# A decoder layer on one Trainium2 core: the MLP's first product as seven half-block products, with weight sums made by adding DMAs

## The chip, the cores and the metric

The kernel runs on one core of a Trainium2 chip. The metric is device microseconds of one execution. In texts and rows PE is TensorE (PEld its weight loads), DVE is VectorE, ACT is ScalarE, POOL is GpSimd and SP is SyncE.

## What is computed

One layer of a hybrid decoder over 512 tokens of width 1024, all in float32: a norm, one wide input projection, sliding-window attention and gated linear attention side by side, their gated merge, an output projection and a residual, then a gated MLP. The change is in the MLP:

```
h = rmsnorm(x, ln_ffn_g)                      # 512 x 1024
a, u = jnp.split(h @ w_ffn_in, 2, axis=-1)    # w_ffn_in 1024 x 5632; a and u 512 x 2816
a = causal_dwconv(a, conv_w, conv_b)          # width 3, along the tokens
x = x + (jax.nn.silu(a) * u) @ w_ffn_out      # w_ffn_out 2816 x 1024
```

## The kernel before

**Products.** Each float32 product is made of float32r parts. A weight chunk is split exactly into `wh` (ACT, L257) and `wl` (DVE, L258), an activation likewise into `acth` and `actl`, and `mm3` (L261) issues three matmuls for each contraction tile of 128: high by high, high by low, low by high. All matmuls are recorded at L80.

**Weights.** A unit of 1 MB goes by SP's queue into a ring `raw` of three buffers (`load`), and is split chunk by chunk into rings `wh` and `wl` of four buffers each. The main loop calls `do_split` for chunks i to i+2 and then issues chunk i's matmuls. PE keeps the order of the text; a scheduler places the instructions of DVE, ACT and POOL by their dependences.

**The MLP's first product.** In `[columns, tokens]` form: weights stationary, 512 tokens moving. A chunk is one column tile of `a` or of `u`, 8 contraction tiles deep, so 24 matmuls; there are 44 chunks, two chunks to a unit. Before it, the last half of the output projection (`mm_o1`) goes block of tokens by block of tokens, each block's norm (L279 to L284) and its transposes (`transpose_steps`, L310 on, L324 the low part) beside the next block's matmuls. The first four chunks (`ffn_first`) take the tokens in two halves of 256, 192 matmuls in all; the other 40 chunks have 960 matmuls of 512 tokens. `evac_fa` (L589 to L599) makes the convolution and the silu of an `a` tile: a memset on POOL (L591), a copy and an activation on ACT (L592, L595), two multiply-adds on DVE (L596, L597), a table lookup on ACT (L86). `evac_fu` (L602) multiplies by the `u` tile into `gT`, eight-KiB slots of four tiles each.

**The MLP's second product.** `fo_chunk(j)` splits `gT(j)` (L640, L641) and accumulates 22 chunks into eight banks (tokens by columns). The last `TAIL` = 4 chunks go bank by bank, so that each bank's addition of the residual (L671) and its store lie beside the next bank's matmuls.

Of the kernel before, what the change touches and what calls it, by code (L numbers as in the profile page):

```python
# [27 lines left out]
STAGES = (32, 8, 2, 1)    # sub-blocks, four to a group; the last ones in pairs  # L28
NEG = -1.0e30


@with_exitstack
def hybrid_trunk(ctx: ExitStack, tc: tile.TileContext, x, ln_mix_g, w_in, q_norm_g, k_norm_g, sinks, w_gk_up,
# [9 lines left out]
    tpool = ctx.enter_context(tc.tile_pool(name="tpool", bufs=1))  # L43
    psum = ctx.enter_context(tc.tile_pool(name="psum", bufs=1, space=bass.MemoryType.PSUM))
# [9 lines left out]
    def slot(name, dt=F32):  # L54
        """An 8 KiB activation slot."""
        return apool.tile([P, 2048], dt, tag="slot", name=nm(name), bufs=10)

    def tmp(shape, name, dt=F32):
        """A short-lived tile from one of three rings, by its size."""
        n = 1  # L60
        for d in shape[1:]:
            n *= d
        tag, size, bufs = ("t0", 16, 12) if n <= 16 else ("t2", 514, 8) if n <= 514 else ("t4", 1040, 3)
# [15 lines left out]
    def matmul(ps, lhsT, rhs, start, stop):  # L79
        order(nc.tensor.matmul(ps, lhsT, rhs, start=start, stop=stop))  # L80
# [3 lines left out]
    def lookup(out, src, func, **kw):  # L84
        """An activation from a table; these keep their order, so that the tables change seldom."""
# [5 lines left out]

    def transpose(ps, src, idn):
# [54 lines left out]
    # the clock of the tensor engine comes up, and stays up, with products of the identity  # L147
# [7 lines left out]
    # the gain of the first norm goes in with the transposes, the norm itself with the products' results  # L155
# [3 lines left out]
    # per-partition parameters: rows in, one transpose  # L159
# [23 lines left out]
    def make_masks():  # L183
        low = ctile([P, P], "low")     # 1 where column <= row
# [3 lines left out]
        upp = ctile([P, P], "upp")     # 1 where column >= row  # L188
# [3 lines left out]
        slow = ctile([P, P], "slow")   # 1 where column < row  # L192
# [28 lines left out]
    def load(u):  # L221
# [4 lines left out]
        t = wpool.tile([P, 2048], F32, tag="raw", name=nm("raw"), bufs=3)[:, :n]  # L226
        t = t.rearrange("p (a b) -> p a b", a=shape[0])
        for dst, src in loads:
            nc.sync.dma_start(t[:, :, dst[0]:dst[1]], src)
        loaded[u] = t  # L230

    split, o1 = {}, []
# [5 lines left out]
    def split_steps(i):  # L238
# [4 lines left out]
        src = loaded[u][:, sl[0], sl[1]]  # L243
# [3 lines left out]
        else:  # L247
            h = wpool.tile([P, 1088], F32R, tag="wh", name=nm("wh"), bufs=4)[:, :n]
            l = wpool.tile([P, 1088], F32R, tag="wl", name=nm("wl"), bufs=4)[:, :n]
        split[i] = h, l = [t.rearrange("p (a b) -> p a b", a=shape[0]) for t in (h, l)]  # L250
        half = shape[0] // 2 if i < 2 else shape[0]
        for k in range(0, shape[0], half):
# [6 lines left out]
            yield  # L259

    def mm3(ps, lh, ll, rh, rl, first, last):  # L261
        matmul(ps, lh, rh, first, False)
        matmul(ps, lh, rl, False, False)
        matmul(ps, ll, rh, False, last)

    def rstd(ss, n, scale, name, r=None):
        """(ss * scale + eps) ** -0.5"""
# [5 lines left out]

    def act_pair(tag):
        h = apool.tile([P, KT, S], F32R, tag=tag + "h", name=nm(tag + "h"), bufs=1)
        l = apool.tile([P, KT, S], F32R, tag=tag + "l", name=nm(tag + "l"), bufs=1)
        return h, l

    def norm(src, gain, out):  # L279
        """out = rmsnorm(src) * gain"""  # L280
# [5 lines left out]
    def mix_steps(b):  # L286
        """hT[:, :, block b] = transpose(x) * gain"""
# [23 lines left out]
    def transpose_steps(h, H, L, b):  # L311
        """H + L [:, :, block b] = transpose(h)"""
        pss = [bank() for _ in range(2)]
        dst = [(slice(None), slice(4 * half, 4 * half + 4), slice(b * P, (b + 1) * P)) for half in range(2)]
# [5 lines left out]
        for d, ps in zip(dst, pss):  # L320
            nc.scalar.copy(H[d], v3(ps, 4))
            yield
        for d, ps in zip(dst, pss):
            nc.vector.tensor_sub(L[d], v3(ps, 4), H[d].bitcast(F32))  # L324
            yield
# [9 lines left out]
    def tok_major(act, key, ncols, kts, first, last, evac):  # L335
        """out[tokens, columns]: activations stationary, weights moving, one bank a block of tokens."""
# [18 lines left out]
    def col_major(act, kt, evac, ncol=1, toks=None):  # L355
        """out[columns, tokens]: weights stationary, activations moving."""
# [18 lines left out]
    act_h = lambda: hT  # noqa: E731  # L375

    # keys, values and low-rank gates of all tokens; then queries of the attention
    zk = slot("zk")[:, 0:NB * 272].rearrange("p (a b) -> p a b", a=NB)
    for u2 in range(2):
        u = unit([((0, 256), win(O_KA, O_QB, 4 * u2, 4 * u2 + 4)),  # L380
                  ((256, 272), win(O_GK, O_GA, 4 * u2, 4 * u2 + 4))], (4, 272))
# [15 lines left out]
    def tok_group(act, key, w, c0, evac):  # L397
        for u2 in range(2):
            u = unit([((0, 512), win(c0, c0 + 512, 4 * u2, 4 * u2 + 4, w))], (4, 512))
# [5 lines left out]
    def col_group(act, w, c0, ntile, evac):  # L405
        """ntile (even) column tiles from column c0; evac(j, ps)"""
        for j in range(0, ntile, 2):
            u = unit([((0, 256), win(c0 + j * P, c0 + (j + 2) * P, 0, KT, w))], (KT, 256))
# [13 lines left out]
    qk = []     # per pair of blocks: q (scaled) of the four heads, then k  # L422
# [42 lines left out]
    # a branch's projection, gated  # L465
    yaT, ybT, mT, h2T = [], [], [], []
    n_a = len(chunks)
    for j in range(0, KT, 4):
        u = unit([((0, 512), win(j * P, (j + 4) * P, 0, 4, w_a))], (4, 512))
# [22 lines left out]
    class Halves:  # L492
        """[P, KT, S] kept as two slots of four tiles each."""

        def __init__(self, pair):
            self.pair = pair

        def __getitem__(self, sl):
            p, k, t = sl
            return self.pair[k // 4][p, k % 4, t]  # L500

# [11 lines left out]
    # the first tiles take the first half of the columns while the second half of them is still on its way  # L513
    def branch_first(i):
        if i < n_rb + 3:
            return
        pss = [bank() for _ in range(4)]
# [13 lines left out]
    act_y = lambda: (Halves([ybT[0][0], ybT[1][0]]), Halves([ybT[0][1], ybT[1][1]]))  # noqa: E731  # L531
    for j in range(0, KT, 2):
        u = unit([((0, 256), win(j * P, (j + 2) * P, 0, KT, w_b))], (KT, 256))
        for c in range(2):
            chunk(u, (slice(0, KT), slice(c * P, (c + 1) * P)), (KT, P), branch_first if j < 4 else
                  col_major(act_y, KT, lambda _, ps, j=j + c: evac_b(j, ps)))

    # output projection and residual
# [572 lines left out]
```

## Time and profile before

| What | Value |
|---|---|
| median of 3 runs | 817.45 us (817.37 to 817.52) |
| span of the profiled execution | 815.8 us |
| PE, DVE, ACT, POOL busy | 99%, 55%, 40%, 13% of the span |
| DMA | 76.87 MB, mean 94 GB/s |

The page gives the span, from the first to the last instruction, and no other time for the profiled execution. The median of the runs lies 1.65 us above the span, and that is taken as what lies around it. Rows of the timeline give the start and the length of an instruction in us; a PE row's length is from issue to the modelled end, so the pace of matmuls is read from the distances of their starts.

### The profile page before, as it was taken

To read this page: it belongs to the slowest core of one execution; us is meant where nothing else is said; L and a number is where in the kernel's file an instruction comes from. 1 tells how busy PE (TensorE), PEld (TensorE's weight loads), DVE (VectorE), ACT (ScalarE), POOL (GpSimd) and SP (SyncE) were. 2 spreads that over 40 slices of the span, in tenths; PEclk is the share of its full clock that TensorE was granted. 3 is DMA by queue.
4 is the path that set the end of the run, shared out by engine and by line. 5 is a ranking of instruction groups with operands and counts; after the bars stand their busy time and mean duration, and the time that the engine had idled before them with its cause. 6 is when DMAs were issued, how large, how long until landed. Compare 5 with 4: busy or idle time off the path is not lost.

```text
span 815.8 us, 9796 instructions
## 1 busy us (share of the span) xinstructions
PE 806.4 (99%) x3854; PEld 673.9 (83%) x3854; DVE 447.6 (55%) x703; ACT 324.8 (40%) x508; POOL 106.0 (13%) x188
## 2 busy tenths in 40 slices
PE   8999999999999999999999999999999999999998
PEld 8888888878788888888888988888888888888886
DVE  5778757765899962556744354434434444433322
ACT  6662433547644432543422243333333334323210
POOL 1521011004757720000000000000000000000000
PEclk9999999999999999999999999999999999999999
DMA  9331231223111321332641033333332223333102
GB/s 319 107 102 54 102 104 53 81 75 104 52 53 51 105 78 53 102 104 82 226 157 52 1 104 104 104 103 104 104 103 94 77 90 102 104 104 103 52 14 90
DMA packets 55952, 76.87 MB, mean 94 GB/s; under 512 B 2636, under 2 KB 42674, under 8 KB 55906
## 3 DMA queue, kind: packets, MB, share of 16 engines
q1 hardware_dynamic: 55794, 76.15, 28.0%
q8 instruction: 30, 0.49, 0.2%
q14 instruction: 16, 0.13, 0.0%
q10 hardware_dynamic: 112, 0.10, 0.0%
HBM read 74.15 MB, written 2.10 MB: 93 GB/s over the span
## 4 chain that ended last, share of the span: by engine, by line
PE 89%; DVE 6%; ACT 2%; POOL 2%; issue 1%; ACTq 0%; POOLq 0%
PE ps L80 86%; PE ps L93 2%; DVE stQ L764 1%; DVE wl L258 1%; ACT acth L296 1%; DVE scr L807 1%; DVE stK L750 1%; ACT bc L86 0%; DVE bc L727 0%; DVE gatea L473 0%; PE warm L80 0%; ACT wh L257 0%; POOL a_r L271 0%; ACT t4a L308 0%; POOL g L698 0%
## 5 line engine op out<-in xcount | busy, mean ns | idle before, releaser
L258 DVE TENSOR_TENSOR wl<-raw,wh 128x1024 fp32r<-128x1024 f32 (+1 forms) x130 | 157.6, 1213 | 155.5 <-ACT wh L257 153.6
L257 ACT CAST wh<-raw 128x1024 fp32r<-128x1024 f32 (+1 forms) x128 | 134.0, 1048 | 256.0 <-PE ps L80 239.9
L80 PE MATMUL ps<-acth,wh 128*128 128x512 f32 (+1 forms) x608 | 234.7, 386 | 0.0
L80 PE MATMUL ps<-acth,wl 128*128 128x512 f32 (+1 forms) x608 | 230.3, 379 | 0.0
L80 PE MATMUL ps<-actl,wh 128*128 128x512 f32 (+1 forms) x608 | 230.1, 378 | 0.0
L80 PE MATMUL ps<-wh,acth 128*128 128x512 f32 (+1 forms) x352 | 132.0, 386 | 0.7 <-ACT acth L296 0.6
L80 PEld LDWEIGHTS ps<-acth,wl 128*128 128x128 f32 x608 | 114.4, 188 | 21.5
L80 PEld LDWEIGHTS ps<-acth,wh 128*128 128x128 f32 x608 | 114.5, 188 | 20.8 <-issue 0.4
L80 PEld LDWEIGHTS ps<-actl,wh 128*128 128x128 f32 x608 | 114.5, 188 | 20.3
L80 PE MATMUL ps<-wl,acth 128*128 128x512 f32 (+1 forms) x352 | 130.4, 381 | 0.1
L80 PE MATMUL ps<-wh,actl 128*128 128x512 f32 (+1 forms) x352 | 130.4, 381 | 0.0
L80 PEld LDWEIGHTS ps<-wh,acth 128*128 128x128 f32 x352 | 64.7, 188 | 13.8 <-ACT acth L296 1.0
L80 PEld LDWEIGHTS ps<-wh,actl 128*128 128x128 f32 x352 | 64.7, 188 | 12.8
L80 PEld LDWEIGHTS ps<-wl,acth 128*128 128x128 f32 x352 | 64.7, 188 | 12.6 <-DVE wl L258 0.6
L769 POOL TENSOR_TENSOR stQ<-stQ,qk 128x128 f32<-128x128 f32 (+2 forms) x80 | 46.5, 610 | 11.1 <-ACT stQ L86 10.4
L602 DVE TENSOR_TENSOR gT<-t2a,ps 128x512 f32<-128x512 f32 x22 | 15.1, 687 | 36.3 <-PE ps L80 35.6
L641 DVE TENSOR_TENSOR actl<-gT,acth 128x512 fp32r<-128x512 f32 x20 | 13.2, 688 | 39.4 <-ACT acth L640 39.4
L764 DVE TENSOR_TENSOR stQ<-bc 128x128 f32<-128x128 f32 (+2 forms) x80 | 32.1, 432 | 0.0
L640 ACT CAST acth<-gT 128x512 fp32r<-128x512 f32 x20 | 11.8, 623 | 46.7 <-PE ps L80 46.7
L591 POOL MEMSET conva<- 128x2 f32 x22 | 2.1, 99 | 214.5 <-DVE t2a L597 169.9
L807 DVE COPY_PREDICATED scr<-smask,ps 128x128 f32<-128x128 uint32 (+2 forms) x80 | 25.6, 324 | 4.9 <-PE ps L80 4.1
L86 ACT ACTIVATE t2a<-t2a 128x512 f32<-128x512 f32 x22 | 13.9, 632 | 33.0 <-DVE t2a L597 32.9
(208 smaller groups left out, 896.6 us busy)
## 6 DMA issues: line engine op xcount, KB each, us to landing
raw<-in_w_in_dram SPq DMA_DIRECT2D x22, 1024.0 KB, 5.1
raw<-in_w_ffn_in_dram SPq DMA_DIRECT2D x22, 1024.0 KB, 5.1
raw<-in_w_ffn_out_dram SPq DMA_DIRECT2D x11, 1024.0 KB, 4.9
raw<-in_w_branch_b_dram SPq DMA_DIRECT2D x4, 1024.0 KB
raw<-in_w_out_dram SPq DMA_DIRECT2D x4, 1024.0 KB, 5.0
x<-in_x_dram SPq DMA_DIRECT2D x4, 512.0 KB, 4.6
raw<-in_w_branch_a_dram SPq DMA_DIRECT2D x2, 1024.0 KB
out_dram<-t2a SPq DMA_DIRECT2D x8, 256.0 KB, 2.0
```

Of the source, the lines that this page charges most:

```text
L80: order(nc.tensor.matmul(ps, lhsT, rhs, start=start, stop=stop))
L86: ins = nc.scalar.activation(out, src, func, **kw).ins
L93: order(nc.tensor.transpose(ps, src, idn))
L257: nc.scalar.copy(h[:, k], src[:, k])
L258: nc.vector.tensor_sub(l[:, k], src[:, k], h[:, k].bitcast(F32))
L296: nc.scalar.mul(hT[0][:, k, tok], ps, g)
L602: nc.vector.tensor_tensor(gT(j), conv.pop(j), ps, ALU.mult)
L640: nc.scalar.copy(H, gT(j))
L641: nc.vector.tensor_sub(L, gT(j), H.bitcast(F32))
L764: nc.vector.tensor_tensor(v[:, :, :, c], Bg[:, hs, :, t], r.broadcast_to([P, 2, P // (per * L), (per - 1 - j) * L]), ALU.subtract)
L769: nc.gpsimd.tensor_tensor(v[:, :, :, c], v[:, :, :, c], qg[:, hs, :, t], ALU.mult)
L807: nc.vector.copy_predicated(Ag[:, :, :, (j + 1) * L:per * L], m.broadcast_to([P, 2, ng, (per - 1 - j) * L]), pg[:, :, :, c])
```

## The change

The 22 pairs of column tiles become 11 groups of two column tiles of `a` and two of `u`. In a group, tokens fall into two halves of 256 and the contraction into two halves of four tiles, so activations are a block matrix (a11, a12; a21, a22), and weights (B11 and B21 of `a`, B12 and B22 of `u`). In place of eight half-block products there are seven, by the form of Strassen's method that Winograd gave, on the operands a11, a12, a22 and the sums s1 to s4. One half-block product is 2 column tiles by 4 contraction tiles by 3 matmuls, each with 256 moving columns.

The activation sums are made once, on DVE, and split (`sums`, `part`). The weight sums are made in place in the `raw` buffer: the unit holds B11 and B22, and after a chunk's split a DMA from POOL's queue with `accum_op=ADD` adds the next block of 512 KB to the half that was split. There are two chains, a11, s1, s2, a22 on the lower half and s4, s3 on the upper. a12's weights, B21, are loaded plainly into a buffer of their own. The table `seq` interleaves the products of neighbouring groups; links of a chain lie four products apart in it. The results are recombined as the banks are read. Beside that: `raw` has four buffers, `wl` three, `t2` seven; x1 (the residual) is written to DRAM after the output projection and read back in the second product; `TAIL` is 3; `gT` tiles are split up to two chunks ahead; the stage of the merge starts with three tiles in place of four. The core of the diff:

```diff
-        t = wpool.tile([P, 2048], F32, tag="raw", name=nm("raw"), bufs=3)[:, :n]
+        t = wpool.tile([P, 2048], F32, tag="raw", name=nm("raw"), bufs=4)[:, :n]
...
-        src = loaded[u][:, sl[0], sl[1]]
+        src = sl() if callable(sl) else loaded[u][:, sl[0], sl[1]]
...
-            l = wpool.tile([P, 1088], F32R, tag="wl", name=nm("wl"), bufs=4)[:, :n]
+            h, l = (wpool.tile([P, 1088], F32R, tag=t, name=nm(t), bufs=n_)[:, :n] for t, n_ in (("wh", 4), ("wl", 3)))
...
+        if i in then:
+            then[i]()
...
+    def sums(b):
+        c = slice(b % 2 * P, (b % 2 + 1) * P)
+        (a11, a12), (a21, a22) = ([t[:, :, c] for t in q] for q in araw)
+        s1, s2, s4, s3 = (tmp([P, 4, P], n) for n in ("s1", "s2", "s4", "s3"))
+        nc.vector.tensor_sub(s1, a21, a22)
+        part("s1", s1, c)
+        nc.vector.tensor_sub(s2, a11, s1)
+        nc.vector.tensor_sub(s4, a12, s2)
+        part("s4", s4, c)
...
+                nc.sync.dma_start(spill[b * P:(b + 1) * P, :], x1(b))
...
+        half = {"a11": lo, "s1": lo, "s2": lo, "a22": lo, "s4": hi, "s3": hi}
+        chain = {"a11": rows[:, lo, cu], "s1": rows[:, hi, cu], "s2": rows[:, hi, ca], "s4": rows[:, lo, cu]}
...
+                for c in range(2):
+                    o, w = ps[:, 256 * c:256 * (c + 1)], slice(c * P, (c + 1) * P)
+                    for k in range(4):
+                        mm3(o, wh[:, k, w], wl[:, k, w], H[:, k, :], L[:, k, :], new and c + k == 0,
+                            (c, k) == (1, 3), not new)
+                evac(a)
...
+            elif a == "s2":
+                nc.vector.tensor_sub(G["v"], G["s2"], G["v"])
+                nc.vector.tensor_add(gj[:, :, 0:256], two(G["s1"]), two(G["v"]))
+            elif a == "s3":
+                nc.vector.tensor_add(G["v"], G["s3"], G["v"])
+                nc.vector.tensor_add(gj[:, :, 256:S], gj[:, :, 256:S], two(G["v"]))
+            elif a == "a22":
+                A = G["a"]
+                nc.vector.tensor_sub(A[:, :, 258:S + 2], two(G["a22"]), two(G["v"]))
...
+                    nc.vector.tensor_mul(gj[:, c, :], gj[:, c, :], t)
...
+                if a in chain:
+                    pool(nc.gpsimd.dma_start(loaded[u][:, half[a], :], chain[a], accum_op=ALU.add))
...
+    for g in range(3, NG - 2):
+        seq += [("a11", g), ("s2", g - 1), ("a12", g), ("s3", g - 1), ("s1", g), ("a22", g - 1), ("s4", g)]
...
-    TAIL = 4
+    TAIL = 3
```

**What moves on PE.** In the middle of the first product, at the seam of two chunks, PE's order was this (`acth_3571` and `actl_3572` are the split activations, `wh` and `wl` the chunk's weights, in which each of the eight contraction tiles is met in turn):

```order
L80 MATMUL ps_4610<-actl_3572,wh_4539 128x512
L80 MATMUL ps_4610<-acth_3571,wl_4540 128x512
L80 MATMUL ps_4610<-acth_3571,wh_4539 128x512
L80 MATMUL ps_4610<-actl_3572,wh_4539 128x512
L80 MATMUL ps_4610<-acth_3571,wl_4540 128x512
```

and at the seam of a product s3 with the next group's s1 (`s_588`, `s_586` their operands, both parts in one slot) it is now:

```order
L84 MATMUL ps_5226<-s_588_3804,wh_5159 128x256 x2
L84 MATMUL ps_5226<-s_588_3804,wl_5160 128x256
L84 MATMUL ps_5258<-s_586_3802,wh_5190 128x256 x2
L84 MATMUL ps_5258<-s_586_3802,wl_5191 128x256
```

A matmul has half the moving columns, and the weights change every 24 matmuls as before; in all 1848 matmuls of 256 stand where 192 of 256 and 960 of 512 stood.

**What moves on DVE.** A pair of column tiles was five instructions, two weight splits together and then the three of the evacuation:

```order
L258 TENSOR_TENSOR wl_723_4955<-raw_703_4814,wh_722_4954 128x1024
L258 TENSOR_TENSOR wl_726_4985<-raw_697_4775,wh_725_4984 128x1024
L596 SCALAR_TENSOR_TENSOR t2a_720_4947<-conva_719_4944,prm_100,t2a_720_4947 128x512
L597 SCALAR_TENSOR_TENSOR t2a_720_4947<-conva_719_4944,prm_100,t2a_720_4947 128x512
L602 TENSOR_TENSOR gT_696_4773<-t2a_720_4947,ps_724_4958 128x512
```

A group, which stands for two such pairs, is now 18 instructions; `raw_673` and `raw_698` are the units of two neighbouring groups, `b21_548` the plain load, `v`, `gT` and `conva` are recombined at L691 to L698:

```order
L691 TENSOR_TENSOR v_734_5157<-ps_761_5395,v_734_5157 128x512
L271 TENSOR_TENSOR wl_763_5423<-raw_698_4819,wh_762_5422 128x1024
L692 TENSOR_TENSOR gT_733_5156<-ps_746_5258,v_734_5157 128x2x256
L271 TENSOR_TENSOR wl_766_5455<-raw_673_4586,wh_765_5454 128x1024
L694 TENSOR_TENSOR v_734_5157<-ps_767_5458,v_734_5157 128x512
L271 TENSOR_TENSOR wl_769_5486<-raw_698_4819,wh_768_5485 128x1024
L695 TENSOR_TENSOR gT_733_5156<-gT_733_5156,v_734_5157 128x2x256
L271 TENSOR_TENSOR wl_773_5520<-raw_722_5051,wh_772_5519 128x1024
L698 TENSOR_TENSOR conva_740_5219<-ps_774_5525,v_734_5157 128x2x256
```

Each product's weight split (now L271) stands alone between two pieces of the evacuation.

**What moves on POOL.** Its queue had only the memsets of L591 in this stage. It now carries the adding transfers of two neighbouring groups in turn, in the order of the text, with one memset a group:

```order
L686 MEMSET conva_715_4986 128x2x2
L718 DMA raw_649_4354<-in_w_ffn_in_dram 128x4x256
L718 DMA raw_673_4586<-in_w_ffn_in_dram 128x4x256
L718 DMA raw_649_4354<-in_w_ffn_in_dram 128x4x256
L718 DMA raw_673_4586<-in_w_ffn_in_dram 128x4x256
L686 MEMSET conva_740_5219 128x2x2
```

Each of these DMAs waits for the split that last read the half it adds to.

## Rows read from the trace of the kernel before

**Rows 1.** The page: span, and busy time of each engine.
```profile
span 815.8 us, 9796 instructions
PE 806.4 (99%) x3854; PEld 673.9 (83%) x3854; DVE 447.6 (55%) x703; ACT 324.8 (40%) x508; POOL 106.0 (13%) x188
```

**Rows 2.** The page: the chain that ended last, shares by engine.
```profile
PE 89%; DVE 6%; ACT 2%; POOL 2%; issue 1%; ACTq 0%; POOLq 0%
```

**Rows 3.** Chain of waits from 440 us on: start, us, what.
```profile
456.12 0.87 PE ps L93 x8
456.99 332.75 PE ps L80 x1533
...
790.85 1.24 DVE wl L258
```

**Rows 4.** Busy time by stretch.
```profile
core 0: us, PE busy (x) PEld busy (x) DVE busy (x) ACT busy (x) POOL busy (x), PEclk, DMA share, GB/s
30.00:434.00 404.00, 401.82 (x1913) 333.83 (x1912) 272.37 (x474) 179.35 (x291) 93.95 (x139) 1.00 0.28 94
210.00:260.00 50.00, 48.22 (x231) 40.98 (x230) 44.90 (x101) 22.33 (x55) 33.68 (x46) 1.00 0.19 62
449.80:473.70 23.90, 23.90 (x201) 23.86 (x201) 9.86 (x13) 9.51 (x13) 0.76 (x5) 1.00 0.01 1
473.70:691.40 217.70, 217.70 (x963) 180.31 (x962) 94.97 (x104) 79.61 (x104) 1.69 (x17) 1.00 0.31 102
691.40:816.00 124.60, 120.42 (x529) 98.85 (x527) 42.54 (x48) 30.39 (x39) 0.00 (x0) 1.00 0.22 76
```

**Rows 5.** Timeline of PE at the seams of the stages: start, us, instruction.
```profile
449.84 0.28 PE L80 MATMUL ps<-acth,wh 128*128 128x256 f32 x1
...
455.83 0.28 PE L80 MATMUL ps<-acth,wl 128*128 128x256 f32 x1
...
473.73 0.40 PE L80 MATMUL ps<-acth,wh 128*128 128x512 f32 x1
...
691.37 0.39 PE L80 MATMUL ps<-wh,gh 128*128 128x512 f32 x1
```

**Rows 6.** Groups by line and shape, 500 to 680 us: count | busy, mean ns.
```profile
L258 DVE TENSOR_TENSOR wl<-raw,wh 128x1024 fp32r<-128x1024 f32 x33 | 40.4, 1225 | 74.0 <-ACT wh L257 72.8
L257 ACT CAST wh<-raw 128x1024 fp32r<-128x1024 f32 x33 | 34.7, 1052 | 89.3 <-PE ps L80 89.3
L595 ACT ACTIVATE t2a<-ps,prm 128x512 f32<-128x512 f32 x17 | 13.3, 783 | 0.0
L596 DVE SCALAR_TENSOR_TENSOR t2a<-conva,prm,t2a 128x512 f32<-128x512 f32 x17 | 12.8, 752 | 0.1
...
L602 DVE TENSOR_TENSOR gT<-t2a,ps 128x512 f32<-128x512 f32 x16 | 11.0, 688 | 29.3 <-PE ps L80 29.3
L86 ACT ACTIVATE t2a<-t2a 128x512 f32<-128x512 f32 x17 | 10.7, 632 | 28.5 <-DVE t2a L597 28.5
L592 ACT COPY conva<-ps 128x512 f32<-128x512 f32 x17 | 9.8, 578 | 0.0
```

**Rows 7.** The page's DMA issues: count, KB each, us from issue to landing.
```profile
raw<-in_w_ffn_in_dram SPq DMA_DIRECT2D x22, 1024.0 KB, 5.1
...
x<-in_x_dram SPq DMA_DIRECT2D x4, 512.0 KB, 4.6
out_dram<-t2a SPq DMA_DIRECT2D x8, 256.0 KB, 2.0
```

**Rows 8.** POOL's groups, 210 to 260 us: count | busy, mean ns.
```profile
L752 POOL TENSOR_TENSOR stK<-stK,qk 128x512 f32<-128x512 f32 x5 | 7.1, 1426 | 5.7 <-ACT stK L86 5.7
```

**Rows 9.** Timeline of DVE at the start of the MLP.
```profile
452.83 1.28 DVE L284 SCALAR_TENSOR_TENSOR h<-x1b,n_r,g 128x1024 f32<-128x1024 f32 x1 [0.73 <-POOL conva L591]
457.21 1.29 DVE L324 TENSOR_TENSOR actl<-ps,acth 128x512 fp32r<-128x512 f32 x2 [3.10 <-ACT acth L321]
```

**Rows 10.** Timeline of weight loads: the last stall before the end.
```profile
792.12 0.19 PEld L80 LDWEIGHTS ps<-wl,acth 128*128 128x128 f32 x1 [0.56 <-DVE wl L258]
```

More of the change, by code (lines that the diff above doesn't have):

```diff
@@ L62, in tmp @@
             n *= d
-        tag, size, bufs = ("t0", 16, 12) if n <= 16 else ("t2", 514, 8) if n <= 514 else ("t4", 1040, 3)
+        tag, size, bufs = ("t0", 16, 12) if n <= 16 else ("t2", 514, 7) if n <= 514 else ("t4", 1040, 3)
         t = tpool.tile([P, size], dt, tag=tag, name=nm(name), bufs=bufs)[0:shape[0], 0:n]
@@ L77, in order, with matmul @@
         return tc.keep_in_program_order(ins)
-    def matmul(ps, lhsT, rhs, start, stop):
-        order(nc.tensor.matmul(ps, lhsT, rhs, start=start, stop=stop))
+    def matmul(ps, lhsT, rhs, start, stop, more=False):
+        order(nc.tensor.matmul(ps, lhsT, rhs, start=start, stop=stop, skip_group_check=more))
     tabled = []
@@ L259, in split_steps, with mm3 @@
             yield
[L261 to L264, printed above, removed]
+        if i in then:
+            then[i]()
+    def mm3(ps, lh, ll, rh, rl, first, last, more=False):
+        matmul(ps, lh, rh, first, False, more)
+        matmul(ps, lh, rl, False, False, more)
+        matmul(ps, ll, rh, False, last, more)
     def rstd(ss, n, scale, name, r=None):
@@ L319, in transpose_steps @@
         yield
[L320 to L325, printed above, removed]
+        for half, ps in enumerate(pss):
+            if b < 2:
+                part(AOP[half], v3(ps, 4), c)
+            nc.scalar.copy(araw[b // 2][half][:, :, c], v3(ps, 4))
+    def sums(b):
+        c = slice(b % 2 * P, (b % 2 + 1) * P)
+        (a11, a12), (a21, a22) = ([t[:, :, c] for t in q] for q in araw)
[5 more added lines that the diff above has]
+        part("s4", s4, c)
+        part("s2", s2, c)
+        nc.vector.tensor_sub(s3, a21, a11)
+        part("s3", s3, c)
+        part("a22", a22, c)
     def run(steps):
@@ L514, in branch_first @@
     def branch_first(i):
-        if i < n_rb + 3:
+        if i < n_rb + 2:
             return
-        pss = [bank() for _ in range(4)]
+        pss = [bank() for _ in range(3)]
         for half in range(2):
@@ new lines, in gT2 @@
+    def gT2(j):
+        gT(j)
+        return gT_s[j // 4][:, j % 4:j % 4 + 2, :]
+    NG = NF // 2
+    groups = [ffn_group(2 * g) for g in range(NG)]
+    seq = [("a11", 0), ("a11", 1), ("a12", 0), ("a11", 2), ("a12", 1), ("s1", 0), ("s1", 1), ("s4", 0), ("a12", 2),
+           ("s4", 1), ("s2", 0), ("s2", 1), ("s3", 0), ("s1", 2), ("s3", 1), ("a22", 0), ("s4", 2), ("a22", 1)]
+    for g in range(3, NG - 2):
+        seq += [("a11", g), ("s2", g - 1), ("a12", g), ("s3", g - 1), ("s1", g), ("a22", g - 1), ("s4", g)]
@@ L629, in hybrid_trunk @@
+    e0, e1, e2 = NG - 3, NG - 2, NG - 1
+    seq += [("a11", e1), ("a11", e2), ("s2", e0), ("a12", e1), ("s1", e1), ("s1", e2), ("s3", e0), ("a12", e2), ("s4", e1),
+            ("s4", e2), ("s2", e1), ("s2", e2), ("a22", e0), ("s3", e1), ("s3", e2), ("a22", e1), ("a22", e2)]
+    assert sorted(seq) == sorted((a, g) for a in AOP for g in range(NG))
+    for a, g in seq:
+        groups[g](a)
     n_fi = len(chunks)
@@ L652, in fo_mm, with fo_ready @@
         matmul(ps, L[:, t], wh[:, 0, w], start=False, stop=j == NF - 1)
+    early = {}
+    def fo_ready(j):
+        for jj in range(j + 1):
+            if jj < NF and jj not in early and jj not in fo:
+                early[jj] = fo_split(jj)
     def fo_chunk(j):
@@ L864, in yb_transpose @@
     def yb_transpose(half):
-        if half:
-            ybT.append([t[:, 0:4, :] for t in act_pair("act")])
-        else:
-            ybT.append([v3(slot(s, F32R), 4) for s in ("ybh", "ybl")])
+        ybT.append([v3(slot(s, F32R), 4) for s in ("ybh", "ybl")])
         H, L = ybT[half]
@@ L1062, in hybrid_trunk @@
         if i == n_o0:
-            h2T.extend(act_pair("act"))
+            aop_tiles(AOP[:2])
+        if i == n_o:
+            aop_tiles(AOP[2:])
+            sums(2)
+        if i == n_o + 3:
+            run(transpose_steps(st["h2"], NB - 1))
+            sums(3)
+        if i == n_fi - 6:
+            fo_ready(1)
+        if i == n_fi + 2:
+            x1s[:] = [slot("x1c"), slot("x1d")]
+            for b in range(NB):
+                nc.sync.dma_start(x1(b), spill[b * P:(b + 1) * P, :])
         if i == n_a:
```

169 lines of the change are left out of this document (105 added, 64 removed).

## The prediction

> **What bounds the kernel now.** I begin with the page: PE is busy for 806.4 of 815.8 us, DVE for 447.6 [rows 1], and PE holds 89% of the chain that ended last [rows 2]. In the part to be changed the chain of waits is one piece of PE, 332.75 us without a break, from the eight transposes of the last block of tokens (0.87 us) to a weight split on DVE close to the end [rows 3]. The table by stretch says the same: in the MLP's first product PE is busy for 23.90 of 23.90 and 217.70 of 217.70 us, DVE for 94.97 and ACT for 79.61 of the latter, DMA has a share of 0.31 at 102 GB/s, and the granted clock is 1.00, the level of 2.4 GHz [rows 4]. So the stage is paced by the number of matmuls times their distance, and everything else has room.
>
> The distance is read from starts [rows 5]. From 449.84 to 455.83 there are 50 steps of 256 columns: 0.120 us each. Over the whole stretch, (473.73 - 449.84 - 0.87) / 192 = 0.120. For 512 columns, (691.37 - 473.73) / 960 = 0.2267. At 2.4 GHz 256 columns are 0.1067 us and 512 are 0.2133, so either kind pays about 0.013 us more than its columns, and a half-width matmul pays it for half the work. In the stretch of half-width matmuls PEld is busy for 23.86 of 23.90 us [rows 4], so weight loads stand back to back there.
>
> **The change, step by step.**
>
> *PE.* Removed: 192 x 0.120 + 960 x 0.2267 = 240.7 us. Added: 77 products x 24 x 0.120 = 1848 x 0.120 = 221.8 us. That is **-18.9 us**. An eighth of the columns goes (30.1 us of 240.7), and the smaller tiles give 11 us of it back. The eight transposes stay. The rule against it or for it: the Trainium skill, "TensorE: Matmul & The Clock Gate", section "Back-to-back issue gap", gives an isolated gap of N / 2.4 + 2.5 ns. By it this term would be (960 x 0.2158 + 192 x 0.1092) - 1848 x 0.1092 = 26.3 us; the rows show five times that overhead, and the measurement decides.
>
> *DVE.* A group takes PE 168 x 0.120 = 20.2 us. In it DVE has seven splits of 1.225, seven additions or products of some 0.69 and four multiply-adds of 0.752 [rows 6]: 8.6 + 4.8 + 3.0 = 16.4 us, or 81%, where two pairs of tiles had 9.3 of 21.9. It stays hidden if its order is good; if this cover went, each us per group over 20.2 would cost 11 us.
>
> *ACT.* Seven casts of 1.052, three copies of 0.578, two activations of 0.783 and two of 0.632 [rows 6]: 11.9 of 20.2 us. Hidden.
>
> *DMA.* At 102 GB/s for a share of 0.31 [rows 4] the 16 engines together would move 329 GB/s. A group loads 1.57 MB plainly, 4.8 us of all engines, and adds four blocks of 0.52 MB, 1.59 us each at the plain rate. If an add costs r times a plain load, a group needs 4.8 + 6.4 r us: 11.1 for r = 1, 17.6 for r = 2, more than 20.2 from r = 2.4 and more than before (240.7 / 11 = 21.9) from r = 2.7. No row of this kernel shows an adding transfer or any from POOL's queue. I take r between 1 and 2, as a read beside each write at most doubles the bytes on the chip's side; hidden.
>
> *The new wait.* An add waits for the split that read its half, the next link's split waits for the add. Behind a waiting add stand the next adds and one memset on POOL; what waits for them in the end is PE. With three buffers `wl`, the split of product p starts when p-3 has ended, two products ahead of its own, and is over 1.5 us later (0.25 of handing over, 1.23 of DVE). Then the add takes L to land, the next split takes 1.05 + 1.23 = 2.3 us, and it has to be there four products further on. So L + 3.8 must be below six products, 6 x 2.88 = 17.3 us: **L up to 13.5 us is free**. The nearest rows: 256 KB land in 2.0 us, four blocks of 512 KB at the start in 4.6, 1 MB in 5.1 [rows 7]. The bounds are 2.0 and 10.2 (twice the megabyte); I take 5, the row of the same size. Even the upper bound is hidden, by 3 us. SP's queue carries the plain loads tens of us ahead of use and the stores of x1 (4 x 512 KB) in a stretch with a DMA share of 0.01 [rows 4]; their reading back goes into one of 0.22. At nothing: their cover is that free share, and without it they would cost 4.6 us each.
>
> *Start of the MLP.* The block that comes last is normed at 454.11, 4.3 us after the stage's start [rows 9]; three products, 8.6 us, come before its transposes, so these do not wait. Then two copies (1.2), a sum, a cast and a split (0.69 + 0.58 + 0.69) and one weight split that stands between (1.23) make the operand s1 at 8.6 + 0.9 + 4.4 = 13.9 us; PE wants it after five products and the transposes, at 15.3. The sums of two blocks are 18 DVE instructions of 0.69, 12.4 us, among the splits; so the slack is small and I take **+0.5** (0 to 1).
>
> *Into the second product.* In the last 17 products (49 us) DVE is about nine tenths full, because the evacuations of three groups and the splits of the first `gT` tiles meet there. The split of the second product's third weight chunk stands behind some 13 evacuation instructions (13 x 0.7 = 9 us); by the order it is ready about one us late. **+1.0** (0 to 2).
>
> *The end.* With three chunks instead of four kept back, the last split lies earlier beside PE's work; the stall of 0.56 us before 792.12 [rows 10], of which 0.23 is the normal pace, goes: **-0.3**. The store of the last bank is the same.
>
> *From 30 to 434 us* PE's order stands; DVE's shifts in places, with three `wl` buffers, and the merge starts with three tiles. PE is idle for 404.00 - 401.82 = 2.2 us of it [rows 4]. Taken as 0, within -2 and +2.
>
> Sum: 815.8 - 18.9 + 0.5 + 1.0 - 0.3 = 798.1 us of span. The median of the runs lies 1.65 us above the span of the profiled execution; with that, **799.8 us**.
>
> **The rivals.**
>
> *A. The adds are too slow (ends slower).* Place: the two chains of a group in `raw`. If L is above 13.5 us, the product's pace is (L + 3.8) / 6, and each us costs 77 / 6 = 12.8 us. At 14.9 the stage lasts as long as before; at 16 it is 77 x 3.3 = 254 us, and the kernel takes 832. If the engines themselves are the limit, the point is r = 2.7, and at r = 3 it is 11 x 24 = 264 us, and 842. For it: no row shows what such a transfer costs, an add must read, add and write each element, and its rows are 1 KB. Against it: landing times of 2.0 to 5.1 us [rows 7], twice of which is still free, and the mean DMA share of 0.31. Chance 0.20.
>
> *B. POOL and DVE exclude each other.* POOL writes the descriptors of its own transfers, and might not get on while DVE works. It would have only what DVE leaves of a group, 20.2 - 16.4 = 3.8 us, or 0.94 per add. If an add takes POOL as long as its nearest row, 1.43 us for 128x512 [rows 8], a group lasts 16.4 + 5.7 = 22.1 us, the stage 243, and the kernel takes about 821; a tenth of a us less per add is 4.4 us less. The point of decision is 0.94 us. Against it: from 210 to 260 us DVE is busy for 44.90 and POOL for 33.68 of 50 us [rows 4], so they overlap for at least 28.6 us. The Trainium skill, "SBUF — State Buffer", section "SBUF: two separate sides", warns of this: a transfer from GpSimd's queue starves while VectorE runs in a mode that takes both of the ports that the two share. No run here has shown such a transfer. Chance 0.05.
>
> *C. The saving comes, but stalls eat a part.* DVE at 81% and in an order made by a scheduler delivers a split late every group, or landing times vary so that some links pass 13.5 us. For it: stalls named above have slacks of 1 to 2 us. One us per group is 11 us; half of it and a us more at either end give 806, in a range of 803 to 819. Against it: between 210 and 260 us, with DVE at 90%, PE still was busy for 48.22 of 50 us [rows 4]. Chance 0.15.
>
> That the change does not do what it says is excluded by the order of instructions: the 1848 matmuls stand there.
>
> **How the numbers follow.** A measurement of this kernel can tell about 0.2%, 1.6 us, from no change. The forecast, with its own range of 796 to 803 from the bounds of the small terms (0 to 1, 0 to 2, -2 to 2), has 0.60. It and nearly all of C (0.13) are faster. The upper end of C (0.02) and the lower of B (0.02) are no change. The rest of B (0.03) and A (0.20) are slower. So 0.73, 0.04, 0.23. The range runs from 796 to 824: it holds the forecast, C, B and the mildest of A, and leaves out most of A, which is a little under 0.2.
>
> **What would show it.** Right: starts of half-width matmuls 0.120 us apart throughout the first product; the stage about 222 us long plus 0.9 for the transposes, with at most 1 or 2 us of PE idle; DVE busy for about 80% of it, ACT 60%; adds from POOL that land in 4 to 10 us; DMA share of 0.5 to 0.9. Small stalls on DVE before s1 and at the start of the second product, none at the last weight split. Wrong: weight casts on ACT that wait for a DMA while PE idles (A), POOL's issues that line up with DVE's gaps (B), PE idle a little in each group behind `wl` (C), or a distance other than 0.120 us, each hundredth of which would move the stage by 18.5 us.

## The result, and the profile after

The changed kernel takes 804.13 us (median of 4 runs, 803.36 to 806.6) where the kernel before takes 817.49: a ratio of 0.9841, interval 0.9826 to 0.9856. The forecast was 799.8, in a range of 796 to 824. So the saving came, 13.4 us of the 17.7 that were expected, and the question is where 4.3 us went. The first lines of the page of the changed kernel, its DMA queues, its chain by engine and its adding transfers:

```profile
span 801.7 us, 11534 instructions
PE 789.6 (98%) x4550; PEld 693.9 (87%) x4550; DVE 524.2 (65%) x805; ACT 371.5 (46%) x566; POOL 161.1 (20%) x221
...
q1 hardware_dynamic: 51490, 74.57, 28.0%
q0 software_dynamic: 23232, 23.07, 19.2%
...
PE 83%; DVE 7%; DMA 3%; POOL 2%; ACT 2%; issue 2%; SPq 0%; ACTq 0%; POOLq 0%; DVEq 0%
...
raw<-in_w_ffn_in_dram POOLq DMA_DIRECT2D x44, 512.0 KB, 6.5
```

Against [rows 1, 2] PE has lost 6 points of the chain, and DMA stands in it with 3%. DVE and ACT are busier by 76.6 and 46.7 us, POOL by 55. The table by stretch, with the MLP's first product cut at 519.3 and 526 us:

```profile
core 0: us, PE busy (x) PEld busy (x) DVE busy (x) ACT busy (x) POOL busy (x), PEclk, DMA share, GB/s
449.40:519.30 69.90, 69.90 (x585) 69.90 (x583) 55.93 (x70) 42.25 (x56) 19.33 (x19) 1.00 0.80 154
519.30:526.00 6.70, 4.16 (x22) 3.96 (x22) 4.21 (x6) 3.90 (x5) 1.77 (x2) 0.75 1.17 250
526.00:672.60 146.60, 146.60 (x1224) 146.60 (x1224) 109.45 (x131) 83.79 (x106) 35.45 (x34) 1.00 0.91 185
672.60:801.70 129.10, 124.22 (x561) 102.48 (x559) 52.56 (x64) 33.85 (x42) 0.00 (x0) 1.00 0.24 82
```

PE is busy without a gap before 519.3 and after 526, as in [rows 4]; between them is one hole, with a granted clock of 0.75 around it. The timeline of PE there, its seam with the second product (the junction), and the one stall of the second product:

```profile
519.25 0.28 PE L84 MATMUL ps<-a,wl 128*128 128x256 f32 x1
522.07 0.64 PE L84 MATMUL ps<-s,wh 128*128 128x256 f32 x2 [2.54 <-ACT gT L689]
...
676.30 0.39 PE L84 MATMUL ps<-wh,gh 128*128 128x512 f32 x1
...
688.73 0.50 PE L84 MATMUL ps<-wl,acth 128*128 128x512 f32 x1 [0.80 <-DVE wl L271]
```

The first product lasts from 449.40 to 676.30, 226.9 us; 221.8 and 0.87 for the transposes were forecast. The hole takes 522.07 - 519.25 - 0.12 = 2.7 us, and until 525.4 the clock is at its lower level and matmuls are some 0.21 us apart, which costs 1.5 us more. Together 4.2 us, all that this stage takes beyond the forecast.

What PE waits for is not a weight: it is the copy at L689, on ACT, of s1's result out of its bank. The product s4 adds into the same bank, so it may not start before the copy. ACT's timeline shows why the copy is late, POOL's shows the transfer in question and the corresponding one of the next group, and the chain of waits (start, us, what) joins the two:

```profile
513.73 1.05 ACT L270 CAST wh<-raw 128x1024 fp32r<-128x1024 f32 x1 [1.83 <-PE ps L84]
514.79 0.59 ACT L687 COPY conva<-ps 128x512 f32<-128x512 f32 x1
520.49 1.04 ACT L270 CAST wh<-raw 128x1024 fp32r<-128x1024 f32 x1 [5.11 <-DMA raw<-in_w_ffn_in_dram]
521.44 0.58 ACT L689 COPY gT<-ps 128x512 f32<-128x512 f32 x1
```

```profile
513.36 1.28 POOL L718 DMA_DIRECT2D raw<-in_w_ffn_in_dram  x1 [9.34 <-DVE wl L271]
...
534.62 1.28 POOL L718 DMA_DIRECT2D raw<-in_w_ffn_in_dram  x1 [10.24 <-DVE wl L271]
```

```profile
511.70 1.14 DVE wl L271
...
513.36 7.03 DMA raw<-in_w_ffn_in_dram
...
520.49 0.07 ACT wh L270
...
521.44 0.59 ACT gT L689
...
522.07 7.99 PE ps L84 x52
```

The cast at 520.49 is that of s2's weights, for a product that begins three products after s1's end, past 525 us. It waited 5.11 us for the add that was issued at 513.36 and landed 7.03 us later, and the copy behind it in the queue waited too. s1's result had been complete at 449.4 + 0.9 + 23 x 2.88 = 516.5. This is **theory Q**: an adding transfer holds up ACT's queue, and what PE misses is an unrelated copy. Its rivals are **theory L** (the chain of split, transfer, split is late in itself, so that weights are missing) and **theory D** (the DMA engines are full).

### The profile page after: what moved, and what is told of

Same layout as the page of the kernel before. It is cut to its first block, busy times and chain, and to the rows that moved or that the text cites. A ratio compares the mean times of both kernels' runs of the same rounds, so it can differ in the third digit from the quotient of the medians.

```text
span 801.7 us, 11534 instructions
## 1 busy us (share of the span) xinstructions
PE 789.6 (98%) x4550; PEld 693.9 (87%) x4550; DVE 524.2 (65%) x805; ACT 371.5 (46%) x566; POOL 161.1 (20%) x221
## 3 DMA queue, kind: packets, MB, share of 16 engines
q0 software_dynamic: 23232, 23.07, 19.2%
## 4 chain that ended last, share of the span: by engine, by line
PE 83%; DVE 7%; DMA 3%; POOL 2%; ACT 2%; issue 2%; SPq 0%; ACTq 0%; POOLq 0%; DVEq 0%
PE ps L84 81%; DMA raw<-in_w_ffn_in_dram 2%; PE ps L107 2%; DVE wl L271 1%; DVE stQ L887 1%; POOL stQ L892 1%; DMA raw<-in_w_in_dram 1%; ACT acth L319 1%; DVE t2a L705 1%; DVE t2a L704 1%; DVE scr L930 0%; DVE gT L707 0%; DVE stK L873 0%; ACT wh L270 0%; ACT t4a L331 0%
## 5 line engine op out<-in xcount | busy, mean ns | idle before, releaser
L271 DVE TENSOR_TENSOR wl<-raw,wh 128x1024 fp32r<-128x1024 f32 (+1 forms) x152 | 186.7, 1230 | 117.3 <-PE ps L84 59.7
L84 PE MATMUL ps<-wh,acth 128*128 128x512 f32 (+1 forms) x352 | 131.9, 385 | 0.5 <-DVE wh L268 0.5
L84 PE MATMUL ps<-s,wh 128*128 128x256 f32 x704 | 129.3, 285 | 2.5 <-ACT gT L689 2.5
L84 PE MATMUL ps<-wl,acth 128*128 128x512 f32 (+1 forms) x352 | 130.3, 381 | 0.8 <-DVE wl L271 0.8
L84 PE MATMUL ps<-wh,actl 128*128 128x512 f32 (+1 forms) x352 | 130.3, 381 | 0.0
L84 PEld LDWEIGHTS ps<-s,wh 128*128 128x128 f32 x704 | 110.2, 192 | 2.7 <-ACT gT L689 2.7
L84 PE MATMUL ps<-s,wl 128*128 128x256 f32 x352 | 100.3, 285 | 0.0
L84 PE MATMUL ps<-a,wh 128*128 128x256 f32 x528 | 96.3, 283 | 0.0
L84 PEld LDWEIGHTS ps<-a,wh 128*128 128x128 f32 x528 | 81.8, 190 | 0.1
L84 PE MATMUL ps<-acth,wh 128*128 128x512 f32 x192 | 79.4, 413 | 0.0
L84 PEld LDWEIGHTS ps<-wh,acth 128*128 128x128 f32 x352 | 64.7, 188 | 13.4 <-issue 1.5
L84 PEld LDWEIGHTS ps<-wl,acth 128*128 128x128 f32 x352 | 64.7, 188 | 13.3 <-DVE wl L271 1.4
L84 PEld LDWEIGHTS ps<-wh,actl 128*128 128x128 f32 x352 | 64.7, 188 | 12.8
L84 PE MATMUL ps<-acth,wl 128*128 128x512 f32 x192 | 75.1, 391 | 0.0
L84 PE MATMUL ps<-actl,wh 128*128 128x512 f32 x192 | 74.9, 390 | 0.0
L84 PE MATMUL ps<-a,wl 128*128 128x256 f32 x264 | 74.7, 283 | 0.0
L84 PEld LDWEIGHTS ps<-s,wl 128*128 128x128 f32 x352 | 67.5, 192 | 0.0
L84 PEld LDWEIGHTS ps<-a,wl 128*128 128x128 f32 x264 | 50.1, 190 | 0.0
L84 PEld LDWEIGHTS ps<-acth,wl 128*128 128x128 f32 x192 | 36.0, 188 | 7.9
```

Of the source, the lines that this page charges most:

```text
L271: nc.vector.tensor_sub(l[:, k], src[:, k], h[:, k].bitcast(F32))
```

## The experiments

Ratios are to the kernel before, in runs on the same chip; each median is of 4 or 5 runs, unless it says otherwise.

**The changed kernel again.** No edit.

> The changed kernel once more, for its spread and as the measure of the runs beside it. Theory Q (a cast on ACT that waits for an adding transfer stands ahead of the copy of s1's result, which the next product s4 waits for): one stall of PE of about 2.7 us near 519 us in a profile with the granted clock at half for some 3 us after it; since the length of the stall hangs on when one transfer lands, runs differ by 1 to 3 us, from about 803 to 806. Theory L (the chain of links itself is late: split, transfer, split): the same stall, and further ones behind wl in other groups. Theory D (the DMA engines are full): landing times grow from group to group, PE idle in many groups.

Measured: 802.99 us (802.26 to 804.1), 0.9823, 0.9810 to 0.9837. One stall, `PE ps L84 <- ACT gT L689` of 2.4 us at the same place, and one of 0.8 before the second product's third chunk. No other group stalls: neither L nor D shows further holes.

**s1's copy ahead of the cast.**

```diff
-                nc.scalar.copy(h[:, k], src[:, k])
+                cast = nc.scalar.copy(h[:, k], src[:, k]).ins
+                if held and held[0] is None:
+                    tc.add_manual_dep(cast, held[1], mybir.DependencyInfo(
+                        mybir.DependencyClass.NoSync, mybir.DependencyReason.DATA), reason="held")
+                    held.clear()
+                elif held:
+                    held.insert(0, None)
...
-                nc.scalar.copy(gj[:, :, 256:S], two(G["s1"]))
+                held[:] = [nc.scalar.copy(gj[:, :, 256:S], two(G["s1"])).ins.name]
```

> The only change is on ACT: the copy of s1's result stands ahead of the cast of s2's weights (one dependence a group); DVE's and POOL's orders are as before. Theory Q: the stall near 519 us goes with the slow clock behind it, 2.7 + 1.5 = 4.2 us: span about 797.5, median about 799.5 to 800, ratio to before about 0.978, and the runs lie closer together than those of the changed kernel. Theory L: s2's weights are no earlier, so PE stalls two products later at the same price: no change, about 804. Theory D: no change.

Measured: 803.48 us (801.35 to 804.63), 0.9825, 0.9812 to 0.9839: no gain in the median, against the expectation of theory Q. The trace, which is that of the 801.35 us run, shows what took its place, in ACT's queue and on PE:

```profile
516.59 0.59 ACT L695 COPY gT<-ps 128x512 f32<-128x512 f32 x1 [1.42 <-PE ps L84]
519.89 1.05 ACT L270 CAST wh<-raw 128x1024 fp32r<-128x1024 f32 x1 [2.72 <-DMA raw<-in_w_ffn_in_dram]
...
526.11 1.05 ACT L270 CAST wh<-raw 128x1024 fp32r<-128x1024 f32 x1 [2.80 <-DMA raw<-in_w_ffn_in_dram]
527.07 1.15 ACT L90 ACTIVATE t2a<-t2a 128x512 f32<-128x512 f32 x2
528.77 1.04 ACT L270 CAST wh<-raw 128x1024 fp32r<-128x1024 f32 x1 [0.56 <-DMA raw<-in_w_ffn_in_dram]
529.73 0.58 ACT L689 COPY v<-ps 128x512 f32<-128x512 f32 x1
```

```profile
530.36 0.51 PE L84 MATMUL ps<-a,wh 128*128 128x256 f32 x2 [2.29 <-ACT v L689]
```

s1's copy (now L695) runs at 516.59, as soon as its product is done, and the hole near 519 is gone. Three products on there is another: a12 of the next group adds into the bank of a11, and a11's copy (now L689) stands behind two casts that waited for adds. It is the same mechanism at the second of the two places where a product adds into a bank that is still to be copied. The edit was right and covered half of it.

**The last groups' evacuation later**, on top of the edit above.

```diff
+                if j >= NF - 4:
+                    late.append(lambda: conv(gj, A))
+                else:
+                    conv(gj, A)
...
+        if i in (n_fi + 4, n_fi + 6):
+            late.pop(0)()
```

> As the run with the copy first, and the last two groups' convolutions and silus (8 multiply-adds, 4 products on DVE) are put behind the weight splits of the second product's first chunks. Theory Q with the junction's term as predicted (a weight split behind some 13 evacuation instructions): the stall of 0.96 us before 688.7 us goes as well, about 1 us less than the run with the copy first: 798.5 to 799. If that stall has another cause (the cast on ACT, the transfer of the weights): no difference from the run with the copy first.

Measured: 801.24 us (799.61 to 801.83), 0.9793, 0.9779 to 0.9806; the run with s1's copy alone had 803.48. Expected were 798.5 to 799. The profile has no stall in the second product and one of 1.8 us behind a11's copy, which the expectation had left out. The two intervals do not meet, but with stalls of 1.8 to 2.5 us that vary from run to run the size of this term isn't settled by this pair.

**Both copies ahead of the casts**, with the late evacuation.

```diff
-                nc.scalar.copy(G["v"], G[a])
+                held[:] = [None, nc.scalar.copy(G["v"], G[a]).ins.name]
```

> As the run with the late evacuation, and the copy of a11's result (the one on which a12 waits, and at which PE stood 1.8 to 2.3 us in the runs with only s1's copy moved) also stands ahead of the casts that wait for adding transfers. Theory Q (a copy that PE needs stands behind a cast that waits for an add): no stall of PE in the first product, which lasts 222.6 to 223 us; span about 796, median 797.5 to 799, runs as close together as those with plain writes (797.8 to 798.6). Theory L (the links are late in themselves): the weights of some later product become the next to stall PE by about 2 us; 801 to 802, as before.

Measured: **798.26 us** (797.86 to 798.5), 0.9762, 0.9748 to 0.9777, the fastest kernel here that computes the whole layer. No row of its trace has PE waiting from 449 us to the end, and the first product lasts from 449.88 to 672.58, 222.7 us, as the forecast had it. Its stretch:

```profile
449.30:672.60 223.30, 223.30 (x1861) 223.12 (x1860) 174.81 (x212) 132.06 (x170) 56.55 (x54) 1.00 0.89 182
```

The landing times are as before (median 6.4 us by the page), and so is the DMA share. Theory Q stands; L, by which the next late weight would have cost as much, falls.

**Both copies without the late evacuation.** The edits of `held` shown above, nothing else.

> Both copies (a11's and s1's) ahead of the casts that wait for adds, the evacuation of the last groups as in the changed kernel. Theory Q: no stall in the first product (222.7 us). What is left is the junction. If its stall of 0.96 us comes from the evacuations ahead of the weight split on DVE, it stays: median 0.5 to 1 us above the run with both copies and the late evacuation, 798.8 to 799.3, with PE waiting for wl near 684 us. If it came from the late adds alone, it goes with them: 798.3.

Measured: 799.1 us (798.89 to 799.19), 0.9775, 0.9761 to 0.9788: 0.84 us over the run before it by the medians (the kernel before, measured beside each, had 817.49 and 817.63), with a PE wait of 0.4 us for wl near 684 (0.6 us lost) and none in the first product, which lasts 222.7 us. So the copies alone take the hole away, and the evacuations ahead of the weight split make a stall of their own. That stall is 0.2 us with only s1's copy moved, 0.4 here and 0.8 in the changed kernel; what sets its length is not shown.

**Plain writes in place of adds.**

```diff
-                    pool(nc.gpsimd.dma_start(loaded[u][:, half[a], :], chain[a], accum_op=ALU.add))
+                    pool(nc.gpsimd.dma_start(loaded[u][:, half[a], :], chain[a]))
```

> The 44 transfers from POOL's queue write the next block in place of adding it (the weight sums are left out, so the output is another one); all waits and orders stay. It tells what the adding costs. By the page, the queue of the adding transfers moved 23.07 MB in 19.2% of the engines' span, 6.7 us a MB, the plain one 74.57 MB in 28.0%, 3.0: if the adding makes the difference, the share in the steady part falls from 0.92 to about 0.5 to 0.6, landing times from 6.5 us to 3 to 5, and under theory Q the stall near 519 us shrinks to under 1 us or goes: 800 to 802. If the cost is that of POOL's queue and its 1 KB rows, share and landing stay as they are. Theory L: the stall shrinks by as much as the landing time. POOL's 1.28 us per transfer stays either way.

Measured: 797.89 us (797.78 to 798.57), 0.9762, 0.9748 to 0.9775. PE waits nowhere from 440 us on, not at the junction either, and the time lies under the 800 to 802 that were expected. Of its page, and of its stretch from 526 us on:

```profile
q0 software_dynamic: 6336, 23.07, 8.7%
...
raw<-in_w_ffn_in_dram POOLq DMA_DIRECT2D x44, 512.0 KB, 4.0
```

```profile
526.00:671.00 145.00, 145.00 (x1211) 145.00 (x1210) 112.06 (x136) 83.70 (x106) 21.00 (x34) 1.00 0.58 189
```

The same 23.07 MB takes 8.7% of 796.0 us in place of 19.2% of 801.7: 3.0 us of all engines per MB against 6.7. **An added byte costs 2.2 times a plain one** here; it comes in packets of 1 KB where the plain one came in packets of 3.6 KB (23232 and 6336 packets), though SP's plain loads take 3.0 us a MB in packets of 1.4 KB, so small packets alone hardly explain it. Landing falls from 6.5 to 4.0 us and the stall is gone: shorter transfers cure it as the order does, as both Q and L expected.

**More bytes.**

```diff
                 nc.sync.dma_start(G["b21"], rows[:, hi, ca])
+                nc.sync.dma_start(G["b21"], rows[:, hi, ca])
```

> The changed kernel with the plain load of B21 done twice (0.52 MB more a group, 1.6 us of all engines at the plain rate). By the queue's shares a group needs 4.8 + 4 x 3.5 = 18.8 us of the engines out of 20.2; with it 20.4. Theory D (the engines are nearly full, so that landing times hang on what else is on them): landing times of the adds rise above 10 us, PE idles in most groups, 806 to 820. Theory Q or L with room on the engines: stalls of the same count as now, 803 to 806.

Measured: 803.98 us (803.01 to 804.71), 0.9836, 0.9819 to 0.9852, no different from the changed kernel. From 526 to 672 us the share rose from 0.91 to 0.97, the adds landed in a median of 6.4 us as before, PE was busy for 145.88 of 146.00 us, and the stalls are the same two (2.2 and 0.8 us). Theory D falls: the engines are not the limit at this load. In the short stretch around the hole the share is even 1.17, so a share near 1 is no sign of its own that the engines are full.

**Half-width matmuls alone**, in the kernel before.

```diff
-                      col_major(act_h2, KT, lambda _, ps, j=j + c, ev=ev: ev(j, ps)))
+                      col_major(act_h2, KT, lambda _, ps, j=j + c, ev=ev: ev(j, ps),
+                                toks=((0, 256), (256, S))))
```

> The kernel before with the first product's other 40 tiles also in two halves of 256 tokens (no seven products): the price of half-width matmuls alone. If a half-width matmul takes 0.120 us: 1920 x 0.120 in place of 960 x 0.2267 is 230.4 - 217.6 = 12.8 us more, 830.2. If it took its columns and 2.5 ns, as for one that stands alone: 1920 x 0.1092 - 960 x 0.2158 = 2.5 us more, 819.9. Nothing else should move.

Measured: 830.53 us (830.28 to 830.81), 1.0157, 1.0142 to 1.0173, which is 12.9 us more than the kernel before, measured beside it, where 0.120 us a matmul gave 12.8. The first product lasts from 450.37 to 704.66, 254.3 us for 2112 matmuls and the transposes, 0.120 each.

**Seven products in a row.**

```diff
+    seq = [("a11", 0), ("a11", 1), ("a12", 0), ("a12", 1)]
+    seq += [(a, g) for g in range(2) for a in ("s1", "s4", "s2", "s3", "a22")]
+    seq += [(a, g) for g in range(2, NG) for a in ("a11", "a12", "s1", "s4", "s2", "s3", "a22")]
```

> The changed kernel with each group's seven products one after the other from the third group on (a11, a12, s1, s4, s2, s3, a22): links two products apart, and a12 and s4 right behind the product whose bank they add to. Theory Q (what PE waits for are the copies out of the banks on ACT): each group shows two stalls of some 0.9 us or more, more where a cast waiting for an add stands ahead; 20 to 40 us more than the changed kernel, 823 to 843. Theory L: a link has 4 products, 11.5 us, for 3.8 + L; with L = 6.5 it just holds, with L = 8 to 10 a product takes 3.0 to 3.45 us, 810 to 845, with PE waiting for wh or wl rather than for copies.

Measured, in one run: 881.43 us, 77 us over the changed kernel, beyond what either theory gave. What PE waited for, and ACT around one of those waits:

```profile
PE ps L84 <- ACT v L683: 35.5, 9, 4.7
PE ps L84 <- ACT gT L689: 20.0, 11, 3.9
```

```profile
643.91 1.99 ACT L270 CAST wh<-raw 128x1024 fp32r<-128x1024 f32 x2 [7.45 <-DMA raw<-in_w_ffn_in_dram]
645.81 1.51 ACT L702 ACTIVATE t2a<-conva,prm 128x512 f32<-128x512 f32 x2
647.23 0.56 ACT L683 COPY v<-ps 128x512 f32<-128x512 f32 x1
```

All 20 of these waits are for the two copies, none for wh or wl, and in ACT's queue the copies stand behind casts that waited for adds; only two of the waits, 0.68 us each, are a copy by itself. I had priced a wait at 0.9 us, the copy alone; with a cast ahead of it the waits for a11's copy average 3.9 us. The rest goes with the granted clock, whose mean is 0.91 from 449 to 740 us. Links of a chain lie only two products apart here, and casts idle up to 8.4 us for their adds, so the adds are late too and this run does not part Q from L. It shows that without the interleaving of groups the copies are what PE meets first.

**One convolution put off**, in the changed kernel, ACT's copies as they were.

```diff
+                if j == 2:
+                    late.append(lambda: conv(gj, A))
+                else:
+                    conv(gj, A)
...
+        if i == n_o + 24:
+            late.pop(0)()
```

> The changed kernel with the convolution of the second group alone put off by some 16 us (4 multiply-adds and 2 products on DVE, 4 instructions on ACT), ACT's copies as they were. It tests why the one stall is at 519 us: in the trace DVE works without a break from 497 to 517 us, since the convolutions of the first two groups fall together, and the weight split of the third group's s1 ends at 512.8, so that its add goes out 0.3 us before that product, where in later groups it goes out 3.4 us before. If this lateness decides: the add goes out about 3 us earlier, the stall near 519 us goes, and either nothing takes its place (about 798.5 to 800) or DVE is as full some 20 us later and the stall comes back one group on at the same length (802 to 804). If the stall hangs on landing times alone: unchanged at 519 us, 803.

Measured: 804.17 us (802.44 to 805.01), 0.9837, 0.9824 to 0.9851. DVE's timeline before the split that the add waits for, in the changed kernel and then in this run:

```profile
510.40 0.69 DVE L707 TENSOR_TENSOR gT<-gT,t2a 128x512 f32<-128x512 f32 x1 [0.63 <-ACT t2a L90]
511.01 0.69 DVE L691 TENSOR_TENSOR v<-ps,v 128x512 f32<-128x512 f32 x1
511.61 1.22 DVE L271 TENSOR_TENSOR wl<-raw,wh 128x1024 fp32r<-128x1024 f32 x1
```

```profile
507.92 0.69 DVE L691 TENSOR_TENSOR v<-ps,v 128x512 f32<-128x512 f32 x1 [1.53 <-PE ps L84]
508.53 1.22 DVE L271 TENSOR_TENSOR wl<-raw,wh 128x1024 fp32r<-128x1024 f32 x1
```

POOL's timeline in this run, and PE's:

```profile
510.04 1.28 POOL L724 DMA_DIRECT2D raw<-in_w_ffn_in_dram  x1 [6.14 <-DVE wl L271]
...
533.93 1.28 POOL L724 DMA_DIRECT2D raw<-in_w_ffn_in_dram  x1 [10.65 <-DVE wl L271]
```

```profile
542.62 0.50 PE L84 MATMUL ps<-s,wh 128*128 128x256 f32 x2 [1.71 <-ACT gT L689]
```

In the changed kernel DVE works from 496.6 us to that split with one pause, of 0.63 us; here it is waiting for PE before it. The add that s2 of the fourth group needs (the expectation counts it as the third) goes out at 510.04 in place of 513.36 and the hole near 519 is gone. Now two convolutions fall together later, DVE's backlog makes a wait of 1.1 us for wl before 529.4, and the next group's add is late: the stall is back one group on, at the same copy. So the one late add comes from a full DVE, as rival C had it, and what turns it into a stall is ACT's order.

## Why the prediction was right, and where it was short

*PE's term was right.* 222.7 us in the run with both copies and in the one with plain writes (449.15 to 671.77, 222.6), against 221.8 + 0.87; the half-width run gives the price of 0.120 us by itself. The Trainium skill gives an isolated gap of N / 2.4 + 2.5 ns ("TensorE: Matmul & The Clock Gate", section "Back-to-back issue gap"). The estimate by it for the half-width run is 819.9 us; that run took 830.5, so the measured 0.120 us decides.

*The new wait: the step that failed.* It said that behind a waiting add stand the next adds and one memset on POOL, and that L up to 13.5 us is free. For the weights that was so: L had a median of 6.5 us, up to 12.4 where four adds go out within nine us near 650, and no split was late for its product in the first product of the changed kernel. But the add has a second waiter, the cast on ACT, and I didn't ask what is queued behind that one. Copies that PE needs stood there: at 519 us, where the add was issued late, 2.7 us and 1.5 of slow clock. With nothing but the two copies put ahead of the casts, the time is 799.1, 0.7 us from the forecast.

*DMA* was mis-sized: r is 2.2, not between 1 and 2, and landing 6.5 us, not 5. By the sum it was still hidden, 18.8 of 20.2 us, and more bytes showed that there was room. The longer landing has its part in the hole all the same: with plain writes, which land in 4.0 us, there is none.

*The start of the MLP* was priced at 0.5 and cost nothing: no run with this order of products shows a stall there. The slack was small, as it said: with seven products in a row s1 comes one product sooner, and PE waits 0.2 and 0.3 us for its operand. *The junction*, priced at 1.0, cost 0.96 (688.73 - 687.54 - 0.23), where it was put: DVE works from 669 us without a break through the evacuations, and the split stands behind them. *The end*: the stall of 0.56 us [rows 10] does not come back; with the four chunks of the kernel before it is there still in the half-width run (0.3 us over the normal pace). But the time after the last matmul's start grew by as much, 801.7 - 797.23 = 4.5 us in place of 815.8 - 811.57 = 4.2. *From 30 to 434 us* nothing changed: PE is busy for 402.34 of 404.00 us.

*Against the span's sum:* 798.1 was forecast and 801.7 profiled. The hole and its clock add 4.2, the end's lost gain 0.3, the start takes off 0.5, and stages begin 0.4 us earlier (449.40 for 449.84): 801.7. The three small errors together take 0.6 us off the miss, which is luck.

*The rivals.* A did not happen. B did not either, though each add kept POOL for 1.28 us, over the 0.94 at which it was to decide: POOL's issue at 513.36 and DVE's split at 513.35 run side by side, the split at its usual 1.22 us, and DVE's split still takes 1220 ns on the mean beside the adds. The warning in "SBUF — State Buffer" of the Trainium skill, section "SBUF: two separate sides", is about VectorE in a mode that takes both shared ports. The traces do not name VectorE's modes, so no run here tests it. C comes nearest, at two thirds of its price (4.3 of 6.2 us over the forecast): a full DVE made one add late. But C had PE wait a little for wl in each group, and what came is one hole behind a copy. The time lies in C's range of 803 to 819, not in the forecast's own of 796 to 803; the stated range holds it because it was drawn to hold C. DVE is busy for 76% of the first product (173.28 of 226.90 us) where 81% was forecast.

What stays open is the spread of the changed kernel's eight runs, 802.3 to 806.6. With both copies ahead of the casts it is 797.9 to 798.5, or 798.9 to 799.2 without the late evacuation, so it belongs to the stall. Part of it goes with the clock: the two runs with a mean granted clock of 1.000 took 802.3 and 802.8 us, the six with 0.997 or 0.998 took 803.2 to 806.6. The traces are of runs of 803.5 and 803.2 us, with holes of 2.5 and 2.4 us and the slow clock behind both; what made 806.6 is not shown.

## What to carry to other kernels

When a change makes an instruction wait for something new, follow every waiter to its own in-order queue and ask what stands behind it there; here the weights came in time, and a copy that had nothing to do with them did not. Where a product adds into a bank that another engine must read first, put that read ahead of anything in its queue that can wait for a transfer. A slack worked out for the mean holds only while the engine that starts the transfer has no backlog: count the seams, where two stages' work falls together, by themselves.

## What was not expected of the hardware

After a hole in PE's work the granted clock fell in some profiles and not in others, and not by the length of the hole. In the five us or so after the restart it is, for the changed kernel (hole of 2.54 us), the run with the late evacuation alone (1.79), the run with s1's copy first (2.29) and the run with more bytes (2.21), in this order:

```profile
522.00:527.00 5.00, 4.93 (x28) 4.93 (x29) 3.83 (x6) 2.71 (x5) 1.29 (x1) 0.66 1.23 199
```

```profile
530.00:535.00 5.00, 4.99 (x29) 4.99 (x30) 2.48 (x4) 1.62 (x2) 1.39 (x2) 0.66 0.48 116
```

```profile
530.20:535.00 4.80, 4.64 (x38) 4.64 (x39) 3.51 (x4) 2.69 (x4) 1.40 (x2) 1.00 0.32 81
```

```profile
522.30:527.00 4.70, 4.61 (x38) 4.61 (x39) 3.78 (x6) 2.88 (x5) 1.29 (x1) 1.00 1.22 198
```

0.66 is a stretch partly at the level of 1.2 GHz, 1.00 is 2.4 GHz throughout. In the second trace of the changed kernel (hole of 2.40 us) it is 0.67 from 521.8 to 527 us; with one convolution put off (hole of 1.71) matmuls are 0.12 us apart from 542.96 us on, 0.34 us after the first. So the hole of 1.79 us drew the lower level and the longer ones of 2.21 and 2.29 did not, and in this kernel a hole of about 2 us has to be priced with 0 or 1.5 us more. An adding transfer also keeps POOL longer: 1.28 us for its issue, against 0.75 for the plain one of the same size, where the expectation had no difference.
